# A row softmax with a position bias: the stores move from SyncE's queue to ScalarE's

## The chip, the cores and the metric

The kernel runs on one core of one Trainium2 chip. The metric is the time of one execution on the device, in microseconds (us): the median of several runs. One more execution was recorded by the hardware profiler, and everything said here of single instructions and single transfers is from that one. VectorE (DVE) and ScalarE (ACT) do the arithmetic. SyncE (SP) only issues transfers between the memory of the chip and the core's on-chip buffers. Sixteen DMA engines carry the transfers out, and every load and store here is spread over all sixteen.

## The reference

For each of 2 x 8 matrices of 2112 x 2112 floats a bias that depends only on the clipped distance of row and column is added, and each row goes through a softmax.

```python
B, H, S = (2, 8, 2112); max_rel = 16
rel = pos[:, None] - pos[None, :]
bias = rel_bias[:, np.clip(rel, -max_rel, max_rel) + max_rel]
logits = logits + bias[None]
exp = np.exp(logits - logits.max(axis=-1, keepdims=True))
return exp / exp.sum(axis=-1, keepdims=True)
```

Input and output are 285.5 MB each, and each is moved once.

## The kernel before

The 33,792 rows are dealt to 128 partitions, 264 consecutive rows to each. A chunk is 6 rows of every partition (`R = 6`): 128 x 50,688 bytes, 6.49 MB. There are 44 chunks and 4 buffers `X[0]` to `X[3]` (`NBUF = 4`), used in turn, and the work is done in place: chunk n is loaded into buffer n mod 4, changed there, stored from there, and then chunk n + 4 may be loaded. The order of everything is written by hand, with a program and semaphores for each engine:

- **VectorE** (loop at L191). For four chunks at a time it copies a strip of the bias into `F` (L160). Then for each chunk it waits for the load (`ld[b]`), and for each of the six rows adds the bias and takes the negated maximum in one instruction (L166, `add`), raising `added`. Then, for each half of the chunk, it waits for three exps (`expd`), takes reciprocals of the row sums (L183) and multiplies the three rows (L187, `scale`), raising `scaled` once a row. Only then does it begin the next chunk's adds.
- **ScalarE** (loop at L197). For each row it waits for one `added` and does the exp with its row sum (L175, `exps`). Its one transfer is the load of the bias table at the beginning (L97).
- **SyncE.** It issues chunk 0 as six loads of a row each (L88), then the loads of chunks 1 to 3 (L78), then store 0 (L82, `store`, which waits for six `scaled`). In its loop (L204) it does, for each chunk n: wait until chunk n + 1 is scaled, issue store n + 1, wait until store n has landed (`st[b]`), issue load n + 4 into the buffer that is now free. At the end come the last stores; that of chunk 43 is issued in two halves of three rows, the first as soon as its rows are scaled (L211, L212).

Loads and stores are thus issued on one queue, SyncE's, and the DMA engines take them up in the order load n + 3, store n + 1, load n + 4, store n + 2. A wait of the form `take(engine, semaphore, n)` (L74) waits for n and takes them off again.

Of the kernel before, what the change touches and what calls it, by code (L numbers as in the profile page):

```python
# [11 lines left out]
ENG = mybir.EngineType  # L12
# [3 lines left out]
def kernel(  # L16
# [6 lines left out]
    nc = tc.nc  # L23
    P = 128
    B, H, S, S2 = logits.shape
# [3 lines left out]
    ROWS = B * H * S // P  # L29
    PB = S // ROWS  # L30
    assert ROWS * P == B * H * S and PB * ROWS == S and PB == H == 8
    R = 6
    NBUF = 4
    STEP = R * NBUF
    N = ROWS // R
    HALF = R // 2
    assert ROWS % STEP == 0
    MW = S + ROWS - 1
# [4 lines left out]
    X = [io.tile([P, R * S], FP32, tag=f"X{b}", name=f"X{b}") for b in range(NBUF)]  # L43
# [9 lines left out]
    def view(t, offset, dims):  # L53

        return bass.AP(tensor=t.tensor, offset=t.offset + offset, ap=[[list(t.ap[0])[0], P]] + dims)

    def rows(t, j, n):

        return bass.AP(tensor=t.tensor, offset=t.offset + j * S, ap=[[ROWS * S, P], [1, n * S]])

    with tc.tile_critical(no_gpsimd_drain=True):
        ld = [nc.alloc_semaphore(f"ld{b}") for b in range(NBUF)]
        st = [nc.alloc_semaphore(f"st{b}") for b in range(NBUF)]
        added = nc.alloc_semaphore("added")
        expd = nc.alloc_semaphore("expd")
        scaled = nc.alloc_semaphore("scaled")
# [6 lines left out]
        def take(eng, sem, n):  # L73
            eng.wait_ge(sem, n).then_inc(sem, -n)  # L74


        def load(j, b):
            nc.sync.dma_start(out=X[b][:, :], in_=rows(logits, j, R)).then_inc(ld[b], 16)  # L78

        def store(j, b, s0=0, n=R):  # L80
            take(nc.sync, scaled, n)
            nc.sync.dma_start(  # L82
                out=rows(out, j + s0, n), in_=X[b][:, s0 * S : (s0 + n) * S]
            ).then_inc(st[b], 16)


        for r in range(R):
            nc.sync.dma_start(  # L88
                out=X[0][:, r * S : (r + 1) * S], in_=rows(logits, r, 1)
            ).then_inc(ld[0] if r == R - 1 else pre, 16)  # L90
        for n in range(1, NBUF):
# [6 lines left out]
            out=rbB,  # L98
            in_=bass.AP(tensor=rel_bias.tensor, offset=rel_bias.offset, ap=[[0, P], [1, H * W]]),
# [27 lines left out]
        for m, op in ((eq, ALU.is_equal), (gt, ALU.is_gt), (le, ALU.is_le), (lt, ALU.is_lt)):  # L127
# [4 lines left out]
            out=view(F, 0, [[W, H], [1, W]]), in0=view(F, 0, [[W, H], [1, W]]),  # L132
# [9 lines left out]
            out=view(F, 0, [[W, PB], [1, W]]), in0=view(F, SC + 2 * PB, [[1, PB], [0, W]]),  # L142
# [7 lines left out]
            out=view(M, U, [[ROWS, PB], [1, W]]), in0=view(F, 0, [[W, PB], [1, W]]),  # L150
            in1=view(F, SC + 8 * PB, [[1, PB], [0, W]]), op=ALU.add))
        then(v.tensor_copy(out=view(M, U + W, [[ROWS, PB], [1, ROWS - W]]),  # L152
                           in_=view(F, SC + 7 * PB, [[1, PB], [0, ROWS - W]])))
# [17 lines left out]
        def exps(b):  # L171
            for r in range(b * R, (b + 1) * R):
                x = X[b][:, (r - b * R) * S : (r - b * R + 1) * S]
                take(nc.scalar, added, 1)
                nc.scalar.activation(  # L175
                    out=x, in_=x, func=EXP, scale=-1.0, bias=nmax[:, r : r + 1],
                    accum_out=tot[:, r : r + 1],
                ).then_inc(expd, 1)

        def scale(b):  # L180
            for r0 in range(b * R, (b + 1) * R, HALF):
                take(v, expd, HALF)
                v.reciprocal(out=rec[:, r0 : r0 + HALF], in_=tot[:, r0 : r0 + HALF]).then_inc(inv, 1)  # L183
                take(v, inv, 1)
                for r in range(r0, r0 + HALF):
                    x = X[b][:, (r - b * R) * S : (r - b * R + 1) * S]
                    v.tensor_scalar_mul(out=x, in0=x, scalar1=rec[:, r : r + 1]).then_inc(scaled, 1)  # L187
# [3 lines left out]
        with nc.Fori(0, ROWS - STEP + 1, STEP, engines=[ENG.DVE]) as j:  # L191
            strip(j)
            take(v, dve, 1)
            for b in range(NBUF):
                add(b)
                scale(b)
        with nc.Fori(0, ROWS // STEP, 1, engines=[ENG.Activation]):  # L197
            for b in range(NBUF):
                exps(b)

        store(0, 0)
        with nc.Fori(0, ROWS - 2 * STEP + 1, STEP, engines=[ENG.SP]) as j:  # L204
            for b in range(NBUF):
                store(j + (b + 1) * R, (b + 1) % NBUF)
                take(nc.sync, st[b], 16)
                load(j + (b + NBUF) * R, b)
        for n in range(N - NBUF + 1, N - 1):
            store(n * R, n % NBUF)  # L210
        store((N - 1) * R, (N - 1) % NBUF, 0, HALF)  # L211
        store((N - 1) * R, (N - 1) % NBUF, HALF, R - HALF)  # L212
        for b in range(NBUF):
            take(nc.sync, st[b], 32 if b == (N - 1) % NBUF else 16)


# [28 lines left out]
```

## Time and profile before

| what | value |
|---|---|
| median of 3 runs | 1331.35 us (1329.97 to 1332.12) |
| profiled execution, own time | 1329.65 us |
| its span, first to last record | 1327.7 us |
| VectorE, ScalarE busy | 976.6 us, 575.2 us |
| bytes moved, mean rate over the span | 571.11 MB, 430 GB/s |
| load of a chunk: issue to landing, median | 44.6 us |
| store of a chunk: issue to landing, median | 52.6 us |

The profile's page gives busy times of the engines, a row of 40 slices of the span with the share in which the DMA engines were busy, the DMA queues with their bytes, and groups of instructions by line. The trace behind it answers finer questions: who waited for whom, the instructions in order of time, the busy share in any stretch, and a record of each DMA packet with its start and duration. A packet here is what one DMA engine moves for one partition of a transfer; an engine has eight of them in each chunk's load or store, and behind them a completion write of 4 bytes. Times are from the start of the span. Busy time says little on which engine sets the end: an engine that waits for a transfer and one that is waited for are both idle at times.

### The profile page before, as it was taken

Reading aid. Unit: us, or ns where it says so; the run is one execution under the profiler, and the core shown is the slowest. Engines: PE = TensorE matmul, PEld = TensorE weight load, DVE = VectorE, ACT = ScalarE, POOL = GpSimd, SP = SyncE. Lnnn points to the kernel's source line nnn. Section 1 sums busy time; section 2 is a strip of 40 time slices with the busy share of each in tenths; the row PEclk is TensorE's granted clock in tenths of the full one; section 3 lists DMA queues with packets and bytes.
Section 4 is the critical chain, followed back from the end, with each engine's and each line's share of the span. In section 5 each row is a group of like instructions: output and inputs, shape, how many; then the busy total and the mean of one; then the engine's idle time right before and its main releaser. Section 6 shows DMA issues by size and latency. Waiting matters only on the chain. (4 is left out here: it accounts for less than half of the span.)

```text
span 1327.7 us, 2454 instructions
## 1 busy us (share of the span) xinstructions
DVE 976.6 (74%) x911; ACT 575.2 (43%) x539; POOL 0.4 (0%) x6
## 2 busy tenths in 40 slices
DVE  6999667777777776687778777677877776687772
ACT  2564333444444343345444333444444343335440
POOL 0000000000000000000000000000000000000000
DMA  9999999999999999999999999999999999999998
GB/s 392 431 428 437 435 420 437 435 434 425 435 437 434 428 435 434 435 429 429 438 438 432 426 438 437 437 425 437 437 437 425 435 440 437 428 432 438 437 426 359
DMA packets 13683, 571.11 MB, mean 430 GB/s; under 512 B 1521, under 2 KB 1649, under 8 KB 1649
## 3 DMA queue, kind: packets, MB, share of 16 engines
q1 hardware_dynamic: 13536, 570.96, 99.6%
q10 hardware_dynamic: 144, 0.14, 0.1%
q14 instruction: 3, 0.02, 0.0%
HBM read 285.61 MB, written 285.47 MB: 430 GB/s over the span
## 5 line engine op out<-in xcount | busy, mean ns | idle before, releaser
L166 DVE CUSTOM_DVE_ANT_0 X<-X,F 128x2112 f32<-128x2112 f32 x264 | 605.2, 2354 | 301.3 <-DVEq L74 301.3
L175 ACT ACTIVATE X<-X,nmax 128x2112 f32<-128x2112 f32 x264 | 541.7, 2052 | 539.3 <-ACTq L74 517.6
L187 DVE TENSOR_SCALAR X<-X,rec 128x2112 f32<-128x2112 f32 x264 | 332.4, 1315 | 13.2
L175 ACT ACT_TABLE_LOAD x11 | 14.1, 1283 | 183.3 <-ACTq L74 183.3
L175 ACT ACTIVATION_READ_ACCUMULATOR X<-X,nmax 128x1 f32 x264 | 49.2, 186 | 0.0
L160 DVE COPY F<-M 128x2135 f32 x11 | 26.1, 2374 | 6.3 <-DVEq L74 6.3
L166 DVE DVE_READ_ACCUMULATOR2_ANT nmax<- 128x1 f32 x264 | 21.7, 82 | 0.0
L183 DVE RECIPROCAL rec<-tot 128x3 f32<-128x3 f32 x88 | 14.9, 170 | 0.0
L131 DVE TENSOR_TENSOR F<-F 128x264 f32<-128x264 f32 x1 | 0.4, 434 | 4.7 <-DMA F<-in_rel_bias_dram 4.7
L152 DVE COPY M<-F 128x1848 f32<-128x1848 f32 x1 | 2.1, 2077 | 0.0
L118 DVE TENSOR_SCALAR ip<-ip 128x8 int32<-128x8 int32 x1 | 0.2, 173 | 1.3 <-POOL ip L102 1.3
L135 DVE TENSOR_REDUCE rbS<-F 128x33 f32<-128x264 f32 x1 | 0.6, 610 | 0.0
L149 DVE TENSOR_TENSOR M<-F 128x264 f32<-128x264 f32 x1 | 0.4, 441 | 0.0
L141 DVE TENSOR_TENSOR F<-F,rbS 128x264 f32<-128x264 f32 x1 | 0.4, 425 | 0.0
L128 DVE TENSOR_SCALAR F<-F 128x8 f32<-128x8 f32 x4 | 0.4, 166 | 0.0
L154 DVE COPY M<-rbS 128x247 f32<-128x247 f32 x1 | 0.4, 408 | 0.0
L139 DVE TENSOR_SCALAR F<-F,rbS 128x8 f32<-128x8 f32 x1 | 0.2, 231 | 0.0
L145 DVE SCALAR_TENSOR_TENSOR F<-F,rbS 128x8 f32<-128x8 f32 x1 | 0.2, 225 | 0.0
L140 DVE TENSOR_SCALAR F<-F,rbS 128x8 f32<-128x8 f32 x1 | 0.2, 222 | 0.0
L146 DVE SCALAR_TENSOR_TENSOR F<-F,rbS 128x8 f32<-128x8 f32 x1 | 0.2, 219 | 0.0
L124 DVE TENSOR_TENSOR F<-ip 128x8 f32<-128x8 int32 x1 | 0.2, 167 | 0.0
L121 DVE TENSOR_TENSOR F<-ip 128x8 f32<-128x8 int32 x1 | 0.2, 166 | 0.0
(9 smaller groups left out, 1.2 us busy)
## 6 DMA issues: line engine op xcount, KB each, us to landing
X<-in_logits_dram SPq DMA_DIRECT2D x43, 6336.0 KB, 44.6
out_dram<-X SPq DMA_DIRECT2D x43, 6336.0 KB, 52.6
X<-in_logits_dram SPq DMA_DIRECT2D x6, 1056.0 KB, 12.1
out_dram<-X SPq DMA_DIRECT2D x2, 3168.0 KB, 21.1
F<-in_rel_bias_dram ACTq DMA_DIRECT2D x1, 132.0 KB, 6.2
```

Of the source, the lines that this page charges most:

```text
L128: then(v.tensor_scalar(out=m, in0=dp, scalar1=0.0, scalar2=None, op0=op))
L131: then(v.tensor_tensor(out=view(F, 0, [[W, H], [1, W]]), in0=view(F, 0, [[W, H], [1, W]]), in1=view(F, SC + 3 * PB, [[1, H], [0, W]]), op= ...
L135: then(v.tensor_reduce(out=rbS[:, :], in_=view(F, 0, [[1, W], [W, H]]), axis=mybir.AxisListType.X, op=ALU.add))
L141: then(v.tensor_tensor(out=view(F, 0, [[W, PB], [1, W]]), in0=view(F, SC + 2 * PB, [[1, PB], [0, W]]), in1=view(rbS, W - 1, [[0, PB], [-1, ...
L149: then(v.tensor_tensor(out=view(M, U, [[ROWS, PB], [1, W]]), in0=view(F, 0, [[W, PB], [1, W]]), in1=view(F, SC + 8 * PB, [[1, PB], [0, W]] ...
L152: then(v.tensor_copy(out=view(M, U + W, [[ROWS, PB], [1, ROWS - W]]), in_=view(F, SC + 7 * PB, [[1, PB], [0, ROWS - W]])))
L154: then(v.tensor_copy(out=M[:, 0:U], in_=low.to_broadcast([P, U])))
L160: v.tensor_copy(out=F[:, :], in_=M[:, bass.ds(ROWS - STEP - j, FW)]).then_inc(dve, 1)
L166: v.tensor_tensor_reduce(out=x, in0=x, in1=F[:, STEP - 1 - r : STEP - 1 - r + S], scale=-1.0, scalar=BIG, op0=ALU.add, op1=ALU.min, accum_ ...
L175: nc.scalar.activation(out=x, in_=x, func=EXP, scale=-1.0, bias=nmax[:, r : r + 1], accum_out=tot[:, r : r + 1],).then_inc(expd, 1)
L183: v.reciprocal(out=rec[:, r0 : r0 + HALF], in_=tot[:, r0 : r0 + HALF]).then_inc(inv, 1)
L187: v.tensor_scalar_mul(out=x, in0=x, scalar1=rec[:, r : r + 1]).then_inc(scaled, 1)
```

## The change

Stores are issued by ScalarE, in its loop, behind the six exps of the same chunk: ScalarE waits until all six rows are scaled, issues the store, and goes on to the next chunk's exps. SyncE's program keeps only the loads and its waits for stores that have landed. The store of the last chunk is no longer halved. The instructions on VectorE are the same and in the same order.

```diff
-        def store(j, b, s0=0, n=R):
-            take(nc.sync, scaled, n)
-            nc.sync.dma_start(
-                out=rows(out, j + s0, n), in_=X[b][:, s0 * S : (s0 + n) * S]
-            ).then_inc(st[b], 16)
+        def store(j, b):
+            take(nc.scalar, scaled, R)
+            nc.scalar.dma_start(out=rows(out, j, R), in_=X[b][:, :]).then_inc(st[b], 16)
...
-        with nc.Fori(0, ROWS // STEP, 1, engines=[ENG.Activation]):
+        with nc.Fori(0, ROWS - STEP + 1, STEP, engines=[ENG.Activation]) as j:
             for b in range(NBUF):
                 exps(b)
-        store(0, 0)
+                store(j + b * R, b)
         with nc.Fori(0, ROWS - 2 * STEP + 1, STEP, engines=[ENG.SP]) as j:
             for b in range(NBUF):
-                store(j + (b + 1) * R, (b + 1) % NBUF)
                 take(nc.sync, st[b], 16)
                 load(j + (b + NBUF) * R, b)
-        for n in range(N - NBUF + 1, N - 1):
-            store(n * R, n % NBUF)
-        store((N - 1) * R, (N - 1) % NBUF, 0, HALF)
-        store((N - 1) * R, (N - 1) % NBUF, HALF, R - HALF)
         for b in range(NBUF):
-            take(nc.sync, st[b], 32 if b == (N - 1) % NBUF else 16)
+            take(nc.sync, st[b], 16)
```

More of the change, by code (lines that the diff above doesn't have):

```diff
@@ L34 @@
     STEP = R * NBUF
-    N = ROWS // R
     HALF = R // 2
```

## The prediction

> **What bounds the kernel now.** I read the page first: busy shares, the slices and the DMA queues. The columns of its third part are packets, MB and the share of the time of the 16 DMA engines.
>
> ```profile
> DVE 976.6 (74%) x911; ACT 575.2 (43%) x539; POOL 0.4 (0%) x6
> ...
> DMA  9999999999999999999999999999999999999998
> ...
> q1 hardware_dynamic: 13536, 570.96, 99.6%
> ```
>
> No compute engine is full, and the transfers are full in every slice. One queue, q1, holds all loads and stores and keeps the engines busy 99.6% of the span. The waits by engine (total, times, longest) agree: VectorE waits for loads, ScalarE waits for VectorE.
>
> ```profile
> DVE X L166 <- DVEq L74: 301.3, 41, 8.8
> ```
>
> Third, the timeline of SyncE's issues. Every 30 us it issues one load:
>
> ```profile
> 126.28 0.35 SPq L78 DMA_DIRECT2D X<-in_logits_dram  x1
> ...
> 549.26 0.35 SPq L78 DMA_DIRECT2D X<-in_logits_dram  x1
> ...
> 1237.05 0.35 SPq L78 DMA_DIRECT2D X<-in_logits_dram  x1
> ```
>
> The first two are 14 chunks apart: 422.98 / 14 = 30.21 us a chunk. The next two are 23 apart: 687.79 / 23 = 29.90 us. The second is the floor. The trace's packet records show why: one chunk is 8 load and 8 store packets of 50,688 bytes for each DMA engine, 10,143 of all 11,008 such packets took 1.872 us, and one starts 1.868 us after the one before it, whether the direction changes or not. 16 x 1.868 us plus two completion writes of 0.006 us is 29.90 us. That is 433.9 GB/s, with no gap to close.
>
> What is lost over this floor is small and visible. 119 packets took more than 1.90 us, 99 of them before 545 us. In the records nearly all of these are last packets of a load, on engines that lag, while the engines ahead have begun the next store. At the change from store to load there are almost none. Each such packet costs its engine 0.03 to 0.8 us, and the engines drift apart: at 545 us, and still at the end, the last of the 16 finishes each transfer 5.6 us after the first, and the mean engine 2.1 us after it. The final windows (span, DVE, ACT, POOL, clock, DMA share, GB/s) show the frayed end:
>
> ```profile
> 1310.00:1320.00 10.00, 0.00 (x0) 0.00 (x0) 0.00 (x0) 1.00 1.01 433
> 1320.00:1328.00 8.00, 0.00 (x0) 0.00 (x0) 0.00 (x0) 1.00 0.27 114
> ```
>
> Full until 1320, then 0.27 x 8 = 2.2 us a mean engine, while the last store ends at 1326.3. So the whole gain open to any reordering of transfers is 5.6 us: a profiled execution of 1329.65 us (span 1327.7, and 1.95 us around it) could become 1324.0. The median of the runs shown is 1331.35, 1.7 us above the profiled execution; I add 1.7 us to each sum, so the floor is 1325.7 us.
>
> **The change, part by part.**
>
> *Bytes and transfers.* Same loads, same stores; the last chunk's two half stores become one, which removes one completion write (0.006 us). 0 us.
>
> *Stores leave SyncE.* In steady state nothing is issued earlier for it. Store 41's issue at 1243.89 us follows the end of that chunk's scaling at 1243.8; the load at 1237.05 follows the landing of store 39 at 1236.5. Both were as early as their data allow. 0 us.
>
> *ScalarE gets 44 waits for six scales and 44 issues.* Behind each wait on ScalarE stand the next chunk's exps, for which VectorE's reciprocals wait. Those exps wait for adds that VectorE does only after these same scales, so the wait adds nothing. The issue itself, 0.41 us by the one DMA that ScalarE issues now (the longest load issue on SyncE is 0.66 us), must fit between the last scale and the first add's result. The tightest place is the start, where VectorE does not wait for loads:
>
> ```profile
> 42.88 2.35 DVE L166 CUSTOM_DVE_ANT_0 X<-X,F 128x2112 f32<-128x2112 f32 x1
> ...
> 45.37 2.05 ACT L175 ACTIVATE X<-X,nmax 128x2112 f32<-128x2112 f32 x1 [8.08 <-ACTq L74]
> ```
>
> The last scale ended about 42.9, the exp began 45.37: 2.4 us of cover for 0.4 to 0.7 us. 0 us; without the cover 44 x 0.41 = 18 us of ScalarE work, which would still fall in the 8 us per chunk (29.9 - 21.8) that VectorE idles.
>
> *Buffers.* With two queues open a load and a store share the engines, so each takes about 2 x 14.95 = 29.9 us. A buffer's round is load 29.9, adds to scales 21.8, store 29.9, some 4 us of issue and landing: 86 of the 4 x 29.9 = 119.6 us available. Loads do not starve. 0 us.
>
> *Start and end.* Store 0 is issued at 43.07 and reaches the engines 1.36 us later (a first load issued at 0.97 starts its packets at 2.33). The loads alone would end at 64.3; 19.9 us of them are left. Sharing, store 0 ends at 74.3, load 3 at 84.2, 9.9 us after it, and this distance stays while both queues are never empty. When load 43 ends, store 41 has had half of 9.9, leaving 10.0, and store 42 has 14.95: 25.0 us of transfers before store 43 is needed. It is ready after landing to first add 0.43, adds to scales 21.8 (1281.81 to 1303.6), issue 0.3 and start 1.36: 23.9 us. It fits by 1.1 us, so the undivided last store costs 0; each us that the distance exceeds 12 costs half a us, bounded at 3.
>
> *Engines that alternate directions.* This is the term that decides, and this trace does not show it directly: each engine will take a load packet, a store packet, a load packet, from two queues. Switching queues costs from 0 (direction change, same queue: 0 in the records) to 0.006 us a packet (the nearest row for something between packets, a completion write): 688 x 0.006 = 4.1 us; I take 0. A negative cost is possible in one way: while a load packet is held up, the engine may move its store packet, and the 5.6 us go. Then the hold-ups. Today the directions are mixed, that is, some engines load while others store, only as long as the engines lag: summed over the 81 changes 392 us. After the change they are mixed from 44 us to about 1290: 1245 us, 3.18 times as long. The mean engine lost 2.1 us in 392; at the same rate it loses 2.1 x 3.18 = 6.7. Keep the last engine's lead over the mean, 5.6 - 2.1 = 3.5 us: 10.2 instead of 5.6 us, **+4.6 us**. From below: -5.6 (no hold-ups). From above: if the last engine's whole lag scales, 5.6 x 3.18 = 17.8, +12.2; if the rate of the first 545 us (29.8 us on 16 engines in 117 us of mixing, 1.6%) never fades, 1245 x 1.6% = 19.8 + 3.5, +17.7. I take the mean engine over the whole run, because it averages the early half with hold-ups and the late half without.
>
> Sum: 1329.65 + 4.6 = 1334.3 profiled, 1336.0 as a median.
>
> The Trainium skill, "DMA: Bandwidth & Descriptors", section "Issuing engines are not separate DMA queues", says that transfers issued by several engines interleave on the same 16 engines and save only issue time. By it the sum would be 1331 us; no run here shows two busy queues yet. The same page's section "Latency and other measured facts" gives 214 GB/s per direction at full rate for copies on the two queues at once. By that figure, 571.1 MB at 428 GB/s, an estimate is 1334 us of transfers where the floor here has 1316: 18 us over the floor, about 1344, against this change.
>
> **Rivals.**
>
> *A, hold-ups vanish.* An engine with two queues fills one's delay with the other. For: packets already overlap by 4 ns. Against: load packets were slow exactly when stores ran elsewhere. 1325.7 us.
>
> *B, no change.* The engines settle into an order in which nothing is held up, as they did after 545 us, where 275 us of mixing cost 20 slow packets. The lag ends near 5.6 us again: 1331.4, and 1328.7 to 1334.
>
> *C, hold-ups never settle and one engine takes them.* Forecast and C are on the slower side; C is one mechanism, a load packet delayed beside other engines' stores, at the rate of the last engine in the first 545 us: 5.6 / 117 = 4.8%. Over 1245 us that is 59.6, so 1385; it decides once the rate stays over 1.6%, above 1350.
>
> *The change does nothing it says* can be left out: the changed program has four stores in ScalarE's loop and loads alone on SyncE.
>
> **How the numbers follow.** A measurement of this kernel tells 0.2%, 2.7 us, from no change. Forecast (1334 to 1350 its own range, 1336 the value): 0.45. A: 0.23. B: 0.22. C: 0.10. Faster 0.23, same 0.22, slower 0.45 + 0.10 = 0.55. The range runs from A less 1.7 us for the spread of runs, 1324, to 1331.4 + 17.7 + 4.1 + 3 = 1356; it leaves out most of C and little else.
>
> **What would show it.** Right: a second queue with about half the bytes; DMA full from 5 to 1300 us; chunk periods between 30.0 and 30.4 us for some hundred us after the start; packets over 1.90 us well above 119; ScalarE's count of exps and their durations unchanged. A: the period 29.90 from the start and a lag under 2 us at the end. C: periods over 30.3 to the end. Wrong in its base: a packet pace other than 1.868 us with both queues open, a gap between packets at queue changes, an idle stretch before the last store over 3 us, or VectorE waiting while the DMA share is below 0.9.

## The result and the profile after

The changed kernel took 1335.43 us, the median of 22 runs; the kernel before, 1330.24 us in 22 runs beside them. The ratio is 1.0029, 95% interval 1.0016 to 1.0042: slower by 0.3%, almost at the 1336.0 us forecast. But the spread says as much as the median. The 22 runs of before lie between 1329.42 and 1332.12 us. Those of the changed kernel lie from 1328.19 to 1338.79 us, in two groups: 5 below 1329.4, none up to 1332, 17 above. The profiled execution, at 1336.78 us (span 1335.0), belongs to the high group.

The page of the changed kernel, the lines that answer to those shown of before: busy times, the DMA slices, and the queues (packets, MB, share of 16 engines).

```profile
DVE 976.7 (73%) x911; ACT 575.1 (43%) x539; POOL 0.4 (0%) x6
...
DMA  9999999999999999999999999999999999999996
...
q1 hardware_dynamic: 7056, 285.48, 49.6%
q10 hardware_dynamic: 6480, 285.61, 49.5%
```

The loads (q1) and the stores with the bias table (q10) now have a queue each, and each fills half of the engines' time. VectorE and ScalarE are as busy as before, so ScalarE's 44 issues disturb nothing. VectorE's waits for loads (total, times, longest) are 311.8 us where they were 301.3:

```profile
DVE X L163 <- DVEq L73: 311.8, 41, 8.9
```

One thing is new: the last slice is only 0.6 full.

The windows of the end show why (span, DVE, ACT, POOL, clock, DMA share, GB/s):

```profile
1290.00:1300.00 10.00, 7.07 (x7) 4.32 (x5) 0.00 (x0) 1.00 1.03 446
1300.00:1310.00 10.00, 9.85 (x10) 8.57 (x8) 0.00 (x0) 1.00 0.59 253
1310.00:1320.00 10.00, 4.57 (x5) 0.00 (x0) 0.00 (x0) 1.00 0.59 253
1320.00:1330.00 10.00, 0.00 (x0) 0.00 (x0) 0.00 (x0) 1.00 0.95 411
```

From 1300 to 1320 us the transfers run at 0.59 of their rate: a hole of 8 us in front of the last store, which is issued at 1314.96. The obvious reading is that the hole is the 7 us by which this span is longer. The packet records say otherwise. 15 of the 16 DMA engines finish store 42 between 1305.4 and 1309.5 and then stand idle. The sixteenth finishes it at 1318.6, 13.2 us behind the first, goes on to store 43 without a gap, and ends at 1333.5. The hole belongs to engines that are early; the end belongs to one that is late.

Where it became late can be read from VectorE's first adds, which start when a load has landed on all engines, that is, on the late one. The timeline of the changed kernel, columns start and duration, and in brackets the idle time before:

```profile
600.14 2.36 DVE L163 CUSTOM_DVE_ANT_0 X<-X,F 128x2112 f32<-128x2112 f32 x1 [6.68 <-DVEq L73]
630.57 2.36 DVE L163 CUSTOM_DVE_ANT_0 X<-X,F 128x2112 f32<-128x2112 f32 x1 [8.63 <-DVEq L73]
661.02 2.36 DVE L163 CUSTOM_DVE_ANT_0 X<-X,F 128x2112 f32<-128x2112 f32 x1 [8.66 <-DVEq L73]
...
904.17 2.36 DVE L163 CUSTOM_DVE_ANT_0 X<-X,F 128x2112 f32<-128x2112 f32 x1 [8.68 <-DVEq L73]
934.09 2.36 DVE L163 CUSTOM_DVE_ANT_0 X<-X,F 128x2112 f32<-128x2112 f32 x1 [8.12 <-DVEq L73]
...
1083.61 2.36 DVE L163 CUSTOM_DVE_ANT_0 X<-X,F 128x2112 f32<-128x2112 f32 x1 [5.81 <-DVEq L73]
1113.51 2.36 DVE L163 CUSTOM_DVE_ANT_0 X<-X,F 128x2112 f32<-128x2112 f32 x1 [8.11 <-DVEq L73]
```

Near 600 us a chunk takes 30.4 us; from 904 us on it takes the floor of 29.90. So the loss is half a microsecond a chunk in the middle of the run, on one engine. The total of all hold-ups over 16 engines, the time of 50,688-byte packets above 1.872 us, is 29.2 us; it was 33.9 in the kernel before. So this profile shows no more hold-ups than before. What differs is where they fall: one engine lost some 12 of the 29 us (it ends 13.2 us behind the first and was 1.4 us behind at the start), where the worst engine of before lost 4.8 of 34 (5.6 us behind, 0.8 at the start).

### The profile page after: what moved, and what is told of

Its sections match the earlier page's. It is cut to its first block, busy times and chain, and to the rows that moved or that the text cites. A ratio compares the mean times of both kernels' runs of the same rounds, so it can differ in the third digit from the quotient of the medians.

```text
span 1335.0 us, 2481 instructions
## 1 busy us (share of the span) xinstructions
DVE 976.7 (73%) x911; ACT 575.1 (43%) x539; POOL 0.4 (0%) x6
## 5 line engine op out<-in xcount | busy, mean ns | idle before, releaser
L163 DVE CUSTOM_DVE_ANT_0 X<-X,F 128x2112 f32<-128x2112 f32 x264 | 605.2, 2355 | 311.8 <-DVEq L73 311.8
L184 DVE TENSOR_SCALAR X<-X,rec 128x2112 f32<-128x2112 f32 x264 | 332.5, 1315 | 13.2
```

Source lines behind the costliest of these rows:

```text
L163: v.tensor_tensor_reduce(out=x, in0=x, in1=F[:, STEP - 1 - r : STEP - 1 - r + S], scale=-1.0, scalar=BIG, op0=ALU.add, op1=ALU.min, accum_ ...
```

## The experiments

Three theories. **Mixing**, the recorded one: load packets are held up because other engines store at the same time, and more mixing holds up the mean engine more. **Tail**: the hole in front of the undivided last store is the cost. **Laggard**: the end is that of the one engine that lags most, whatever the total.

### Last store in halves again (h1)

```diff
+        store(ROWS - R, NBUF - 1, 0, HALF)
+        store(ROWS - R, NBUF - 1, HALF, R - HALF)
```

> The changed kernel with the last chunk's store halved again, each half on ScalarE's queue as soon as its three rows are scaled. Tail theory (the 0.59 DMA share from 1300 to 1320 us, in front of the undivided last store, is what the change costs): the first half starts 4 us earlier, the hole shrinks, and the median falls by 3 to 5 us, from 1335.4 to about 1331. Laggard theory (one DMA engine ends 13 us behind the others and has no hole in front of its last store): the median stays at 1335.4 within 1.5 us. Mixing theory (the recorded one, hold-ups on the mean engine): also no change.

Median 1329.32 us in 11 runs (1327.64 to 1334.36), ratio to before 0.9994, 0.9984 to 1.0004. Alone this looks like the tail theory's gain. But the unchanged copy run beside it (h4, below) gave the same, so halving the last store has no visible part in it.

### The kernel before with a whole last store (h2)

```diff
-        for n in range(N - NBUF + 1, N - 1):
+        for n in range(N - NBUF + 1, N):
             store(n * R, n % NBUF)
-        store((N - 1) * R, (N - 1) % NBUF, 0, HALF)
-        store((N - 1) * R, (N - 1) % NBUF, HALF, R - HALF)
```

> The kernel before with one undivided last store, the other part of the change alone. Laggard and mixing theories: 1330.2 within 1 us, as store 43 is ready 8 us before the queue reaches it. Tail theory: the whole store is ready 4 us later than the first half was, which the 11 us of queue in front of it cover, so also 1330 to 1331; more than 1332 would say that an undivided store costs something by itself.

1331.98 us, and before 1331.31 beside it; ratio 1.0003, 0.9994 to 1.0011. This part of the change costs nothing, as forecast.

### One queue, directions changed half as often (h3)

```diff
+            for b in (0, 2):
+                store(j + b * R, b)
+                store(j + (b + 1) * R, b + 1)
+                for c in (b, b + 1):
+                    take(nc.sync, st[c], 16)
+                    load(j + (c + NBUF) * R, c)
```

> The kernel before with one queue, but two stores and then two loads in turn, so that the direction changes half as often (about 20 changes from load to store where there were 41). If each change from load to store brings its hold-ups (mixing theory), the last engine's lag falls from 5.6 us to about 3 and the median from 1330.2 to about 1327.5. If the engines drift apart until they no longer disturb each other, whatever the number of changes (settling), the lag ends near 5.6 us again and the median at 1330 within 1 us.

1332.3 us, ratio 1.0009, 1.0000 to 1.0017. The profiled execution, at 1334.44 us the slowest of its 11, had 51 us of hold-ups, and its last engine was 10 us behind. The 33.9 us of the kernel before come from another session; beside h3, h2 with the usual order had 47 us and a lag of 5.6. So half as many changes of direction brought no fewer hold-ups and no smaller lag: neither expectation was met, and the mixing theory in its simple form finds no support here.

### The changed kernel again (h4, and k1 in another session on another chip)

> The changed kernel once more, for a second profile. Laggard theory: the run's time is 1323.6 us (1320.3 us of floor for an engine that is never held up, 1.5 us to the span's end and 1.8 us around the span) plus the lag of the last engine, whatever that lag is this time, and most other engines end in a hole in front of store 43; the total of all hold-ups stays near 30 us over 16 engines. Mixing theory: a total well above the 34 us of the kernel before, over 60 us. Tail theory: the time follows the hole of the other engines and not the last engine's lag.

h4: median 1328.86 us in 12 runs, 9 of them below 1329.2 and 3 above 1334; ratio 0.9995, 0.9979 to 1.0011. Beside the kernel before, no cost shows here. The profile's hold-ups were 11.2 us: far below the 60 of the mixing theory, and not near 30 as the laggard theory had them. The windows of h4's profiled execution, from the low group:

```profile
1300.00:1310.00 10.00, 6.41 (x7) 0.81 (x2) 0.00 (x0) 1.00 0.91 390
1310.00:1320.00 10.00, 0.00 (x0) 0.00 (x0) 0.00 (x0) 1.00 0.95 411
1320.00:1330.00 10.00, 0.00 (x0) 0.00 (x0) 0.00 (x0) 1.00 0.20 86
```

The hole is down to about 1.5 us a mean engine, with the last store still whole and the last engine 5.1 us behind: in these profiles a smaller lag goes with a smaller hole.

> The changed kernel a third time, as the control of the three beside it. By its 34 runs so far its times fall in two groups, 1327.4 to 1330 and 1332 to 1339 us; both are expected again, in unknown shares. Its time minus 1323.6 us should again be the lag of the last engine in the profile.

k1: median 1335.42 us in 12 runs (1327.28 to 1338.66), 8 above 1332, one between the groups at 1331.08; ratio 1.0026, 1.0007 to 1.0044. Its profiled execution caught a lag in the making. First adds, k1:

```profile
743.82 2.36 DVE L163 CUSTOM_DVE_ANT_0 X<-X,F 128x2112 f32<-128x2112 f32 x1 [8.11 <-DVEq L73]
773.77 2.36 DVE L163 CUSTOM_DVE_ANT_0 X<-X,F 128x2112 f32<-128x2112 f32 x1 [8.15 <-DVEq L73]
...
863.97 2.36 DVE L163 CUSTOM_DVE_ANT_0 X<-X,F 128x2112 f32<-128x2112 f32 x1 [8.11 <-DVEq L73]
894.16 2.36 DVE L163 CUSTOM_DVE_ANT_0 X<-X,F 128x2112 f32<-128x2112 f32 x1 [8.40 <-DVEq L73]
...
1016.10 2.36 DVE L163 CUSTOM_DVE_ANT_0 X<-X,F 128x2112 f32<-128x2112 f32 x1 [8.91 <-DVEq L73]
1046.03 2.36 DVE L163 CUSTOM_DVE_ANT_0 X<-X,F 128x2112 f32<-128x2112 f32 x1 [8.14 <-DVEq L73]
1076.85 2.36 DVE L163 CUSTOM_DVE_ANT_0 X<-X,F 128x2112 f32<-128x2112 f32 x1 [6.74 <-DVEq L73]
...
1290.56 2.36 DVE L163 CUSTOM_DVE_ANT_0 X<-X,F 128x2112 f32<-128x2112 f32 x1 [8.94 <-DVEq L73]
```

A chunk takes 29.95 us near 750; (1016.10 - 863.97) / 5 = 30.43 us from 864; (1290.56 - 1046.03) / 8 = 30.57 after 1046. From about 890 us on, one engine's loads land 0.3 us later with each chunk, then 0.8, and from 863 to 1016 us its loads fall from 3.1 to 5.7 us behind those of the first engine.

Beyond 5.5 us of lag a second thing can be seen. Load n + 4 is issued only when store n has landed on every engine, and the records show loads ending 7.5 us behind the store of three chunks earlier, of which about 2 us go for landing, issue and start. So beyond 5.5 us the early engines have no load to work on and take store packets instead: the lag of the loads stays between 5.3 and 5.8 us while the stores of the early engines run ahead (by 15.9 us for store 40), and these engines end in the hole.

This accounts for the hole. It is not shown to be why the one engine loses time: here its steady loss began at a lag of 3.1 us, and in the first profile of the changed kernel at 1.4 us and steadily at 2.8, when the loads of the other engines were still on time. There the loss also ended, at 904 us, while the stores of the earliest engine were still over 20 us ahead.

Four profiles together say where the time goes. The last engine's lag is that behind the first one at the end of the store in front of the last; 1323.6 us is 1320.3 for an engine never held up, 1.5 to the end of the span and 1.8 around it.

| profile | all hold-ups, us | last engine's lag, us | 1323.6 + lag | own time, us |
|---|---|---|---|---|
| before | 33.9 | 5.6 | 1329.2 | 1329.65 |
| changed, first | 29.2 | 13.2 | 1336.8 | 1336.78 |
| changed, h4 | 11.2 | 5.1 | 1328.7 | 1328.77 |
| changed, k1 | 29.4 | 10.5 | 1334.1 | 1334.39 |

In the profiles of h1 (above) and of g1, k2 and k3 (below), with lags of 5.1, 3.6, 5.7 and 6.6 us, the sum is within 0.3 us of the own time; in those of g2, h2 and h3 it is 0.7 to 1.4 us short. So the laggard sets the end, as that theory has it. The sum says where the time goes and not what holds the engine up.

### More distance between loads and stores (g1, k2, k3), and less (g2)

In g1 stores 0 and 43 are halved; k2 is the same kernel on the other chip; k3 halves store 0 alone. In g2 store 0 is issued one exp later.

```diff
+            if b == 0:
+                store(0, 0, 0, HALF)
+                store(0, 0, HALF, R - HALF)
```

```diff
+        exps(0)
+        exps(1, 0, 1)
+        store(0, 0)
+        exps(1, 1)
```

> The changed kernel with store 0 in two halves, the first 4 us earlier, so that loads end about 16 us after the store of three chunks earlier where they ended 7.5 us after it (d in the trace), and the last store in two halves as before, so that no hole opens at the end. Dry-queue theory (once one engine lags by more than d less 2 us, the other engines' load queues run dry, they only store, and the lagging engine's loads are held up every chunk until its lag is 13 us): the lag may now reach 14 us without that, the high runs of 1334 to 1339 us go, all runs lie between 1327 and 1331, the median is 1328.5, 2 to 3 us below the kernel before on this chip. Rival (one engine's loads are held up for a reason that has nothing to do with the other queues): one run in four or more is again above 1333.

1326.88 us in 6 runs (1326.85 to 1327.56), before 1331.58 beside it: ratio 0.9969, 0.9957 to 0.9981, the best of all, with 8.6 us of hold-ups. The changed kernel itself was not run beside these. The distance, though, became 9.1 us and not 16: the halves were served at a third of the rate, see the last section.

> The changed kernel with only store 0 issued 4 us later, behind the first exp of chunk 1. Loads then end with, or less than 2 us after, the store of three chunks earlier, and the next load is always issued too late: the load queue runs dry in every chunk from the start. Dry-queue theory: hold-ups on lagging engines from the first chunks on, the total of all hold-ups over 30 us, nearly all runs between 1333 and 1339, median 1336. Rival: the same two groups as the changed kernel had on this chip or the other, most runs near 1329.

1329.13 us in 11 runs, one above 1332 (1334.02, the profiled one). A clear miss. One late load at the start restored the distance, to 14 us for the first engine, and later loads were hardly ever late; so the kernel never was in the state that it was meant to test. Its profile tells against the dry-queue theory all the same: with loads ending 14 us behind the stores, one engine's loads fell from 3.8 to 8.3 us behind those of the first between 359 and 962 us, and the hold-ups came to 43.8 us.

> The kernel with stores 0 and 43 in halves again. In the profile the first store in halves made the load queue run dry once at the start, after which loads ended 9.4 us behind the stores instead of 7.5. If that wider distance keeps the lagging engine out of the runaway: all runs between 1326.5 and 1330, median 1327, none above 1331. If six runs without a high one were luck: two or more of some ten runs above 1332.

Median 1328.16 us in 12 runs, but 3 between 1336 and 1339: ratio 0.9999, 0.9979 to 1.0018. g1's gain did not repeat.

> The changed kernel with only store 0 in halves, the last store whole. If the start alone decides: no runs above 1331, and 0 to 2 us more than with both halved, for the hole in front of the last store, which the wider distance makes longer: 1327 to 1329. If the halved last store was what helped: two groups as in the changed kernel.

Median 1328.9 us in 12 runs, again 3 above 1336: ratio 1.0006, 0.9987 to 1.0025. Of the runs taken together with k1, 6 of 24 with store 0 halved were above 1332, and 8 of 12 without. A wider distance may make a runaway rarer; it does not prevent it, and these counts are too small to call the first part shown.

### Transfers alone (g3, g4, k4)

g3 and k4 leave out all arithmetic and store each chunk as it was loaded, on one queue and on two; g4 has 44 loads and only four stores.

```diff
+        def put(j, b):
+            take(nc.scalar, ld[b], 16)
+            nc.scalar.dma_start(out=rows(out, j, R), in_=X[b][:, :]).then_inc(st[b], 16)
```

> No arithmetic and only the last four stores: 44 loads in a row on one queue. If hold-ups need stores on other engines: under 3 us of them in total over 16 engines, each load 14.95 to 14.99 us, and a span of 23 + 43 x 14.96 + 4 x 14.95 = 726 us, give or take 2. If loads are held up by themselves: 15 us or more in total, half of what 44 chunks show today.

725.47 us, and not one packet above 1.90 us; the last engine 0.4 us behind the first. Counted as in the table, as time above 1.872 us, the total is 20.2 us and misses the 3 us expected, but all of it is small: 1.876 us is the most common packet time here, and the longest packet took 1.895. What puts single engines far behind, packets held up by up to 1 us (the longest took 2.90 us in the first profile of the changed kernel), is not there without stores beside the loads. With two queues store packets are held up as well: 30 of the 126 slow packets in the first profile of the changed kernel, 23 of 48 in h4.

> No arithmetic: the kernel before with its loads and stores alone, each chunk stored as it was loaded, in the same order on one queue. If the arithmetic's access to the buffers has no part in the hold-ups: 34 us of hold-ups in total or more, on last packets of loads, and a last engine's lag of about 5.6 us, some 1330 us. If it has: under 10 us in total, lag under 2 us, 1324 to 1326.

1330.78 us, the median of 8 runs, with 51.5 us of hold-ups and a lag of 7.1 us in the profiled one. With no arithmetic at all the hold-ups are those of the full kernel or more, so they do not need the buffer accesses of VectorE and ScalarE. Three of the 8 runs lie between 1335.55 and 1336.43 us: one queue can have a high group too.

> No arithmetic: the changed kernel's loads on SyncE's queue and stores on ScalarE's, each chunk stored as it was loaded, as soon as its load has landed. If arithmetic has no part in the lag of one engine: two groups again, the low one near 1325 to 1329, the high one above 1332, and hold-ups of 9 to 30 us in total, fewer than the 51.5 of the copy on one queue. If arithmetic is what disturbs one engine: one narrow group and under 9 us of hold-ups.

1340.28 us in 9 runs, seven of them between 1325.18 and 1343.28 and two at 1352.94 and 1378.9; ratio without these two 1.0042, 1.0016 to 1.0068. The profiled one, at 1343.28, has 250 us of hold-ups. Both expectations missed, by far. What differs in the records is the distance of the two streams: loads end 52.3 us behind the store of three chunks earlier, not 7.5. With so much distance no load queue is near empty, yet one engine fell from 0.9 to 4.8 us behind between 165 and 498 us: an empty load queue is not needed for it. Slices from k4's page, GB/s:

```profile
GB/s 387 435 435 435 435 434 435 434 435 434 432 435 428 431 434 429 434 435 431 434 434 435 432 434 431 435 431 431 431 428 425 432 432 429 432 414 388 394 396 337
```

Full for the first quarter with both queues open, and then decaying. So mixed directions can be had at 435 GB/s, and can also cost much; how much seems to depend on which packets of the two streams meet. That the distance makes it worse is argued from this one kernel, which differs in more than the distance, and not shown.

## Why the prediction was right, and where only its number was

- **What bounds the kernel, and what is free.** Right. A packet follows another after 1.868 us with both queues open, and the records show loads and stores taken in turn. No cost shows for ScalarE's waits and issues, SyncE's shorter program or the whole last store (h2).
- **The floor and the term that decides.** Right: the time over the floor is, to within some tenths of a microsecond, the last engine's lag. 10.2 us was forecast; the three profiles of the changed kernel have 13.2, 10.5 and 5.1.
- **How that lag was made up.** Wrong in both parts, which cancelled. "The mean engine lost 2.1 us in 392; at the same rate it loses 2.1 x 3.18 = 6.7": it lost 29.2 / 16 = 1.8 us, and 0.7 in h4. "Keep the last engine's lead over the mean, 5.6 - 2.1 = 3.5 us": it was 13.2 - 1.8 = 11.4. Hold-ups did not grow with the time that directions are mixed: 29.2, 11.2 and 29.4 us in the three profiles, where 3.18 times 33.9 would be 108. The near hit of the median is partly luck.
- **One value for two groups.** The forecast was a single case with rivals. The kernel does both: the low group (1327 to 1330) lies between the rivals A and B, the high group (1332 to 1339) is the forecast's, and which one makes the median differed by session: 17 of 22, 3 of 12 and 8 of 12 runs above 1332. The sign "slower" holds for the first measurement and for k1, not for h4.
- **The end.** The distance of loads from stores was forecast as 9.9 us and was 7.5, so store 43 would have fitted by more. One term of it was off: the first packet of store 0 started 3.6 us after its issue at 43.75, where 1.36 was reckoned. It did not fit for 15 engines, because the landing of load 43 waits for the sixteenth. The forecast's check "an idle stretch before the last store over 3 us" was hit, yet the halved store (h1) gained nothing over h4.
- **Signs to look for.** "packets over 1.90 us well above 119": 126, 128 and 48. "chunk periods between 30.0 and 30.4 us for some hundred us after the start": by VectorE's first adds from 115 us on, the mean of ten chunks is 30.28 in the first profile, but 29.95 in h4 and 29.97 in k1. Later it is 30.39 until 904 us in the first profile, and 30.5 from 864 us in k1.
- **The rules that were weighed.** The Trainium skill, "DMA: Bandwidth & Descriptors", "Issuing engines are not separate DMA queues", expects a second issuing engine to save issue time alone; the unchanged pace of 1.868 us agrees. The 214 GB/s per direction of the same page's "Latency and other measured facts" is for copies of 16 KiB a partition between HBM tensors; the estimate of 1344 us carried it over to this kernel, and this case does not agree: the first profile of the changed kernel moves 433 to 437 GB/s in 26 of its 40 slices.

**Left open:** why it is one engine that is held up, by half a microsecond a chunk; what begins this, and what ends it, as at 904 us in the first profile; whether the second queue brings it about, since the totals are no higher with it and the copy on one queue (g3) has a high group too; and why it happens more often in one session than in another. The sessions differ in chip and in time, so the chip is not shown to be the reason.

## What to carry to other kernels

When a kernel moves bytes at the DMA engines' own pace, as here, moving stores to another queue does not make the transfers faster; look at when each of the 16 engines finishes, for the last one is the kernel's time, and a hole in the mean DMA share may belong to the fifteen that are early. Take several runs and look at their groups before explaining a median difference of 0.3%, and run the unchanged kernel beside every experiment: h1 alone would have seemed to prove a theory that h4 takes away. A sum that comes out right does not show that its terms were right: check each against the trace.

## What the runs showed that was not expected

- **A queue of smaller packets gets less.** In g1 the first half store (packets of 25,344 bytes, 0.94 us) shared the engines with a load (50,688 bytes, 1.87 us). It was issued at 39.57 us:

```profile
39.57 4.35 ACTq L81 DMA_DIRECT2D out_dram<-X  x2
```

On the engine that was first, its packets started at 43.11, 45.92, 48.73 and 51.53 us, 2.81 us apart, with a load packet between each two: 0.94 + 1.87 = 2.81. So one packet of each queue was taken in turn, though one was twice as long, and the store got a third of the time. The Trainium skill, "DMA: Bandwidth & Descriptors", "Queues, rings and completion order", says that an engine goes round its queues a packet at a time, and counts some 9 to 17 descriptors to a packet. Here the turn changed after each packet of the trace, which is one partition's piece of a transfer; whether the page means the same by a packet, no run here shows.
- **Loads in a row are a little slower than loads between stores.** 14.984 us each in g4, 14.951 us in the kernel before: 1.876 us was the most common packet time in g4, 1.872 in the others. By this a change of direction costs nothing.
- **Two queues can be steadier than one.** In its low group the changed kernel has a third of the hold-ups of the kernel before (11.2 us in h4's profile against 33.9) and comes down to 1327.3 us, 1.6 us below the best run of before in any session (1328.87).
